# A decoder layer's down projection: results formed in place, twelve slots in reserve, one tile of f split per step, chunks of 10, 12, 12 and 10 row tiles

## The chip, the cores and the metric

The kernel runs on one core of one Trainium2 chip. The metric is the device time of one execution in microseconds; the time before is the median of three runs, 2716.6 us (2716.36 to 2725.06). A difference of about 0.3% is what a measurement of this kernel can tell from none.

## The reference, cut to what matters

One layer of a decoder: a normalised and modulated input, two attention branches with gates, an output projection, then a feed-forward part. The change touches the feed-forward part and a routine which the gates use too. In float32, with 512 tokens, a width of 2048 and an inner width of 5632:

```python
u = h @ w_up                                   # (512, 2048) @ (2048, 11264)
conv = b_conv + sum(w_conv[j] * up[:, j:j + S])  # causal, three taps
gate, val = split(conv)
f = silu(gate) * val                           # (512, 5632)
x = x + gt_f * (f @ w_down)                    # (512, 5632) @ (5632, 2048)
```

The kernel holds everything transposed: rows are channels (128 partitions), columns are the 512 tokens.

## The kernel before, in words

**Numbers as hi and lo.** A float32 matrix is multiplied as three products of rounded halves. `split` (L114, L115) makes them: ACT writes `hi`, a rounded copy, and DVE writes `lo`, the source less `hi`. Each weight tile and each operand tile goes through it. For one pair of K slabs PE then does hi x hi, hi x lo and lo x hi (L1065, L1066, L1067).

**Seven products for eight.** Gates, up projection (except its first group) and down projection run in `seven`, a scheme with seven block products in place of eight. A `Pair` is two output tiles of 128 rows and 512 tokens, computed as a 2 x 2 block of (row tile) x (token half); K is the number of row tiles in each half of the inner dimension. The seven steps have the order p1, p7, p6, p2, p5, p4, p3, and each has an operand set of K blocks of 128 x 256: r11, t3, t2, r21, t1, t4, r22 (`KINDS`). The weights of a pair are four blocks, loaded by SP into five `raw` buffers (in most of the up projection partly into slots), combined by DVE (`comb`, L965) and split into three `whi`/`wlo` buffers. The weights of a step are prepared two steps ahead (`AHEAD`).

**Evictions.** A pair has two PSUM banks of 512 columns, used as three halves X, Y and Z. p1 starts X, p6, p5 and p3 add to X; p7 starts Y, p4 adds to it; p2 uses Z. After each step its half is read: e1, e7, e6 and e3 are copies by ACT (`copy`, L969 with the per-row factor of the down projection, L971 without), e2, e5 and e4 are additions by DVE (`plus`, L975 and L977). Before, e1 and e7 write the two halves of a scratch tile `s` and e6 half of another one, `s6`; e2, e5 and e4 read them and write `u1` and `u2`.

**Slots.** Operands, f, results and scratch live in 81 tiles of 128 x 512, handed out by `get` from the front of a queue and returned by `put` to its end. The order in which they are handed out is fixed when the program is written; an instruction that writes a slot waits for the slot's last readers. A result tile of the down projection is read by an accumulating DMA into `x1_d` (L1526, issued by POOL); in the last chunk it is added to x1 (L1523) and stored.

**f and its chunks.** The up projection yields f, 44 row tiles. For two of them `f_out` computes the sums that the scheme needs and writes them to DRAM (L1373, L1382). The down projection goes over f in four chunks, `DH` = 6, 6, 5, 5 pairs of row tiles, and in each chunk over eight pairs of output tiles, so 56 steps a chunk. A chunk needs seven sets. A set is DH blocks of 128 x 256 in three tiles (with five blocks the third tile is half full), loaded by SP (`load_set`, L1459, one DMA per block) and split into six slots, which stay until the set's last use in the chunk's last pair.

**What sets the order.** After each step `hook` returns the operands that have had their last use and calls `ahead`, which splits and loads sets of the next chunk. `split_set` splits all three tiles of a set. It does so when at least 2 n + 8 slots are free (n is 3; 6 in place of 8 for the first chunk), at every fourth step for the first four sets of a chunk, and at any step in the last eight steps before the chunk is needed. Loads are written while fewer than three sets wait and n + 8 slots are free. The program's text is not the order of the queues: a planner orders each engine's instructions by its own model of time, so an instruction can stand in its queue ahead of ones that are written earlier. Each engine then runs its queue in that order.

## Time and profile before

| | |
|---|---|
| median of three runs | 2716.6 us (2716.36 to 2725.06) |
| profiled execution | 2718.77 us, its span 2716.3 us, mean granted clock 0.99 |
| PE busy | 2620.4 us (96%) |
| DVE busy | 2184.6 us (80%) |
| ACT busy | 1285.3 us (47%) |
| POOL busy | 270.5 us (10%) |
| DMA | 464.33 MB, mean 171 GB/s |

A row of a group of instructions gives line, engine, operation, names of output and inputs, shapes and count, then busy time and the mean duration of one in ns, then the idle time of the engine just before them with what ended it. A row of waits says who waited for what: us in total, times, longest. A row of the timeline gives start and length in us, engine, line, operation, names, and in brackets the idle time before it. A row of a stretch gives for each engine the busy time and the number of instructions in it. `x<-slot` is the accumulating DMA of a result tile, `slot<-f` a load of f.

### The profile page before, as it was taken

What the parts mean: (1) busy time and instruction counts of PE and PEld (TensorE: products, weight loads), DVE (VectorE), ACT (ScalarE), POOL (GpSimd) and SP (SyncE); (2) the same over time, 40 slices, a digit from 0 to 9 for tenths busy, and PEclk for the clock granted to TensorE, in tenths of its full rate; (3) what the DMA queues carried; (4) which work ended last, traced back from release to release, by engine and by line L of the source; (5) the groups of instructions that cost most, each with busy time, mean ns of one, the idle gap of its engine ahead of it and who ended that gap; (6) DMA issues with size and microseconds to landing.
All of it is one profiled execution on the core that took longest, in us unless ns stands there. A gap on an engine that the chain in (4) does not pass through costs nothing. (4 is left out here: it accounts for less than half of the span.)

```text
span 2716.3 us, 45517 instructions
## 1 busy us (share of the span) xinstructions
PE 2620.4 (96%) x17200; PEld 2351.7 (87%) x17200; DVE 2184.6 (80%) x3669; ACT 1285.3 (47%) x2069; POOL 270.5 (10%) x495
## 2 busy tenths in 40 slices
PE   6999999998999999999999999999999989898999
PEld 5777687778997767788789999999999989898989
DVE  7877966688878667983778989989889897777778
ACT  4333434334444455332545555555555464545554
POOL 1001011110032222110100000000000001011110
PEclk8999899999999999999999999999999999999999
DMA  9943136664585578962333333433433466766574
GB/s 343 341 153 98 34 110 213 197 214 156 190 269 164 161 255 288 323 238 93 132 114 124 134 137 113 147 120 114 148 120 128 140 205 154 187 141 173 137 206 125
DMA packets 236241, 464.33 MB, mean 171 GB/s; under 512 B 24331, under 2 KB 85413, under 8 KB 236021
## 3 DMA queue, kind: packets, MB, share of 16 engines
q1 hardware_dynamic: 199348, 368.79, 42.5%
q0 software_dynamic: 36640, 92.63, 11.7%
q8 instruction: 134, 2.20, 0.3%
q14 instruction: 87, 0.70, 0.1%
q10 hardware_dynamic: 32, 0.01, 0.0%
HBM read 397.11 MB, written 64.23 MB: 170 GB/s over the span
## 5 line engine op out<-in xcount | busy, mean ns | idle before, releaser
L1065 PE MATMUL bank<-slot,whi 128*128 128x256 f32 x3920 | 1109.9, 283 | 49.4 <-ACT slot L969 17.0
L1067 PE MATMUL bank<-slot,wlo 128*128 128x256 f32 x3920 | 1101.6, 282 | 8.3 <-DVE wlo L115 8.2
L1066 PE MATMUL bank<-slot,whi 128*128 128x256 f32 x3920 | 1104.4, 282 | 0.4 <-DVE slot L115 0.4
L1065 PEld LDWEIGHTS bank<-slot,whi 128*128 128x128 f32 x3920 | 743.4, 190 | 62.4 <-ACT slot L969 22.2
L1067 PEld LDWEIGHTS bank<-slot,wlo 128*128 128x128 f32 x3920 | 739.9, 189 | 10.8 <-DVE wlo L115 10.3
L1066 PEld LDWEIGHTS bank<-slot,whi 128*128 128x128 f32 x3920 | 741.7, 189 | 0.8 <-DVE slot L115 0.6
L114 ACT ACTIVATE whi<-raw 128x1024 fp32r<-128x1024 f32 (+2 forms) x458 | 424.6, 928 | 500.1 <-PE bank L1066 385.5
L115 DVE TENSOR_TENSOR wlo<-raw,whi 128x1024 fp32r<-128x1024 f32 (+2 forms) x458 | 482.1, 1056 | 61.7 <-ACT whi L114 59.6
L106 ACT ACTIVATE whi<-raw 128x1024 fp32r<-128x1024 f32 (+4 forms) x182 | 187.3, 1032 | 396.0 <-PE bank L120 201.8
L107 DVE TENSOR_TENSOR wlo<-raw,whi 128x1024 fp32r<-128x1024 f32 (+4 forms) x182 | 215.7, 1186 | 146.4 <-ACT whi L106 146.0
L965 DVE TENSOR_TENSOR raw<-raw,raw 128x1024 f32<-128x1024 f32 (+2 forms) x252 | 264.8, 1051 | 61.8 <-DMA raw<-in_w_down 33.3
L119 PE MATMUL bank<-wlo,slot 128*128 128x512 f32 (+2 forms) x768 | 297.4, 388 | 0.9 <-DVE wlo L107 0.9
L118 PE MATMUL bank<-whi,slot 128*128 128x512 f32 (+2 forms) x768 | 290.1, 391 | 4.7 <-ACT slot L385 4.3
L120 PE MATMUL bank<-whi,slot 128*128 128x512 f32 (+2 forms) x768 | 293.3, 385 | 0.0
L118 PE MATMUL bank<-slot,whi 128*128 128x512 f32 (+1 forms) x656 | 261.2, 405 | 3.3 <-ACT slot L1346 2.3
L119 PE MATMUL bank<-slot,whi 128*128 128x512 f32 (+1 forms) x656 | 263.1, 402 | 0.7 <-DVE slot L687 0.7
L120 PE MATMUL bank<-slot,wlo 128*128 128x512 f32 (+1 forms) x656 | 257.5, 401 | 0.0
L118 PEld LDWEIGHTS bank<-whi,slot 128*128 128x128 f32 x768 | 145.9, 190 | 36.1 <-ACT slot L385 4.3
L723 DVE SCALAR_TENSOR_TENSOR slot<-slot,c_act,slot 128x512 f32<-128x512 f32 x203 | 148.9, 745 | 33.9 <-DMA slot<-in_w_ada 32.8
L119 PEld LDWEIGHTS bank<-wlo,slot 128*128 128x128 f32 x768 | 146.2, 190 | 30.0 <-DVE wlo L107 1.4
L120 PEld LDWEIGHTS bank<-whi,slot 128*128 128x128 f32 x768 | 144.6, 188 | 29.0 <-issue 0.5
L114 ACT ACTIVATE whi<-slot 128x512 fp32r<-128x512 f32 x204 | 127.0, 630 | 79.4 <-PE bank L1066 63.8
(292 smaller groups left out, 3004.6 us busy)
## 6 DMA issues: line engine op xcount, KB each, us to landing
slot<-in_w_ada SPq DMA_DIRECT2D x344, 256.0 KB, 5.7
raw<-in_w_ups SPq DMA_DIRECT2D x126, 512.0 KB, 4.4
raw<-in_w_in SPq DMA_DIRECT2D x50, 512.0 KB, 3.6
raw<-in_w_down SPq DMA_DIRECT2D x64, 384.0 KB, 3.1
raw<-in_w_down SPq DMA_DIRECT2D x64, 320.0 KB, 3.4
slot<-f SPq DMA_DIRECT2D x154, 128.0 KB, 3.3
slot<-in_w_ups SPq DMA_DIRECT2D x68, 256.0 KB, 2.6
f<-slot POOLq DMA_DIRECT2D x66, 256.0 KB, 5.2
```

The source lines that it names most:

```text
L106: A.activation(hi, raw[:, :w], AF.Copy)
L107: V.tensor_tensor(lo, raw[:, :w], r32(hi), ALU.subtract)
L114: A.activation(dst_hi, src, AF.Copy)
L115: V.tensor_tensor(dst_lo, src, r32(dst_hi), ALU.subtract)
L118: PE.matmul(o, lh, rh, start=first, stop=False)
L119: PE.matmul(o, lh, rl, start=False, stop=False)
L120: PE.matmul(o, ll, rh, start=False, stop=last)
L723: V.scalar_tensor_tensor(acc, ts[i], c_act[:, k:k + 1], acc, op0=ALU.mult, op1=ALU.add)
L965: V.tensor_tensor(part(o, x, y), part(a, x, y), part(b, x, y), op)
L1065: PE.matmul(o, wh[:, ks], rh, start=first and k == 0, stop=False, skip_group_check=True)
L1066: PE.matmul(o, wh[:, ks], rl, start=False, stop=False, skip_group_check=True)
L1067: PE.matmul(o, wl[:, ks], rh, start=False, stop=last, skip_group_check=True)
```

## The change

Four things change together.

- `seven`: the scratch tiles `s` and `s6` are gone. e1 takes `u1` and copies X into its left half, e7 takes `u2` and copies Y into its right half, e6 copies into the left half of `u2`; e2, e5 and e4 add to these halves in place.
- `split_set` becomes `split_tile`, which splits one tile.
- `ahead` splits a tile at every third step, and at each of the last eight steps before the chunk and the first steps of it, when 14 slots are free (8 for the first chunk). It splits a second tile in a step when otherwise some set would come too late. Loads need n + 12 free slots. The window opens 54 steps before the chunk instead of 50.
- The chunks are 5, 6, 6 and 5 pairs of row tiles; the host packs w_down accordingly.

```diff
-    DH=(6, 6, 5, 5),
+    DH=(5, 6, 6, 5),
...
-            def plus(o, b, g, x):
+            def plus(o, b, g):
                 if g is not None:
-                    V.scalar_tensor_tensor(o, b, g, x, op0=ALU.mult, op1=ALU.add)
+                    V.scalar_tensor_tensor(o, b, g, o, op0=ALU.mult, op1=ALU.add)
                 else:
-                    V.tensor_tensor(o, b, x, ALU.add)
+                    V.tensor_tensor(o, b, o, ALU.add)
...
             def e1():
-                E["s"] = get()
-                copy(E["s"][:, :HT], X, g1)
+                E["u1"] = get()
+                copy(E["u1"][:, :HT], X, g1)

             def e7():
-                copy(E["s"][:, HT:], Y, g2)
+                E["u2"] = get()
+                copy(E["u2"][:, HT:], Y, g2)

             def e6():
-                E["s6"] = get()
-                copy(E["s6"][:, :HT], X, g2)
+                copy(E["u2"][:, :HT], X, g2)

             def e2():
-                E["u1"] = get()
-                plus(E["u1"][:, :HT], Z, g1, E["s"][:, :HT])
+                plus(E["u1"][:, :HT], Z, g1)

             def e5():
-                E["u2"] = get()
-                plus(E["u2"][:, HT:], X, g2, E["s"][:, HT:])
-                put(E["s"])
+                plus(E["u2"][:, HT:], X, g2)

             def e4():
-                plus(E["u2"][:, :HT], Y, g2, E["s6"][:, :HT])
-                put(E["s6"])
+                plus(E["u2"][:, :HT], Y, g2)
...
-    def split_set():
-        c, n, ts = coming.popleft()
-        for i, t in enumerate(ts):
-            hi, lo = getr(), getr()
-            w = min(T, (DH[c] - 2 * i) * HT)
-            split(hi[:, :w], lo[:, :w], t[:, :w])
-            put(t)
-            held_by[c][n] += [hi, lo]
-            ops[c][n] += [(hi[:, o:o + HT], lo[:, o:o + HT]) for o in range(0, w, HT)]
+    def split_tile():
+
+        c, n, ts = coming[0]
+        t = ts.pop(0)
+        if not ts:
+            coming.popleft()
+        w = T if ts or DH[c] % 2 == 0 else HT
+        hi, lo = getr(), getr()
+        split(hi[:, :w], lo[:, :w], t[:, :w])
+        put(t)
+        held_by[c][n] += [hi, lo]
+        ops[c][n] += [(hi[:, o:o + HT], lo[:, o:o + HT]) for o in range(0, w, HT)]
...
-        if c > last or left > 50:
+        if c > last or left > 54:
             return
-        n, spare = need(c), 8 if c else 6
-        if coming and coming[0][0] <= c and len(free) >= 2 * n + spare and (left <= 8 or left % 4 == 0 and made[0] < 4):
-            made[0] = (made[0] + 1) % 7
-            split_set()
-        while todo and todo[0][0] <= c and len(coming) < (3 if c or len(free) > 15 else 1) and len(free) >= n + spare:
+        spare = 12 if c else 6
+        near = left <= 8
+        if coming and len(free) >= 2 + spare and (near or left % 3 == 0):
+            split_tile()
+
+            n = (DH[c] + 1) // 2
+            at = KINDS.index(coming[0][1]) if coming else 7
+            if any(len(coming[0][2]) + n * (i - at) > left + i - 2 for i in range(at, 7)):
+                split_tile()
+        while todo and todo[0][0] <= c and len(coming) < (3 if c or len(free) > 15 else 1) \
+                and len(free) >= (DH[c] + 1) // 2 + spare:
             load_set()
...
-        ahead(0 if (coming or todo or [(0,)])[0][0] == c else 56 - r, c + 1)
+        ahead(-r if (coming or todo or [(0,)])[0][0] == c else 56 - r, c + 1)
```

More of the change, by code (lines that the diff above doesn't have):

```diff
@@ L1460, in load_set @@
         coming.append((c, n, ts))
-    def split_set():
-        c, n, ts = coming.popleft()
-        for i, t in enumerate(ts):
-            hi, lo = getr(), getr()
-            w = min(T, (DH[c] - 2 * i) * HT)
-            split(hi[:, :w], lo[:, :w], t[:, :w])
-            put(t)
-            held_by[c][n] += [hi, lo]
-            ops[c][n] += [(hi[:, o:o + HT], lo[:, o:o + HT]) for o in range(0, w, HT)]
-    def need(c):
-        return (DH[c] + 1) // 2
-    made = [0]
+    def split_tile():
[9 more added lines that the diff above has]
+        ops[c][n] += [(hi[:, o:o + HT], lo[:, o:o + HT]) for o in range(0, w, HT)]
     def ahead(left, last):
         c = (coming or todo or [(9,)])[0][0]
-        if c > last or left > 50:
+        if c > last or left > 54:
             return
-        n, spare = need(c), 8 if c else 6
-        if coming and coming[0][0] <= c and len(free) >= 2 * n + spare and (left <= 8 or left % 4 == 0 and made[0] < 4):
-            made[0] = (made[0] + 1) % 7
-            split_set()
-        while todo and todo[0][0] <= c and len(coming) < (3 if c or len(free) > 15 else 1) and len(free) >= n + spare:
+        spare = 12 if c else 6
[8 more added lines that the diff above has]
+                and len(free) >= (DH[c] + 1) // 2 + spare:
             load_set()
@@ L1583 @@
             dn, k0, ds = a.reshape(DFF // (2 * P), 2, P, D), 0, []
-            for n in (6, 6, 5, 5):
+            for n in (5, 6, 6, 5):
                 b = dn[k0:k0 + n].transpose(1, 0, 2, 3).reshape(2 * n * P, D)
```

## The prediction

> **What bounds the kernel now.** I read the page's slices first, then the busy times by stretch, then the waits, then single queues.

> ```profile
> span 2716.3 us, 45517 instructions
> PE   6999999998999999999999999999999989898999
> ```

> PE is at 90% or more in nearly every slice; the visible dents of the second half stand in the last fifth, the down projection. The stretches below are cut at first matmuls, found by counting (a pair of output tiles is 7 products of 3 x 6 matmuls with twelve row tiles, 3 x 5 with ten). Columns: stretch, length, busy time and instructions of PE, PEld, DVE, ACT, POOL, granted clock, DMA share, GB/s.

> ```profile
> 2176.30:2196.20 19.90, 19.90 (x171) 19.90 (x170) 18.28 (x24) 11.85 (x17) 1.62 (x3) 1.00 0.51 159
> 2196.20:2222.40 26.20, 21.94 (x171) 21.53 (x170) 24.30 (x35) 17.13 (x28) 0.54 (x1) 0.93 0.81 249
> 2222.40:2244.40 22.00, 17.76 (x128) 16.79 (x127) 20.60 (x31) 14.16 (x23) 2.51 (x4) 0.92 0.75 241
> 2244.40:2261.80 17.40, 15.65 (x129) 15.17 (x128) 12.03 (x16) 8.01 (x12) 0.87 (x1) 1.00 0.61 170
> 2277.20:2307.00 29.80, 29.80 (x254) 29.80 (x253) 22.94 (x29) 15.38 (x23) 3.50 (x5) 1.00 0.59 142
> 2307.00:2341.70 34.70, 30.92 (x255) 30.10 (x254) 24.51 (x33) 16.31 (x25) 3.30 (x5) 1.00 0.59 145
> 2341.70:2358.60 16.90, 15.15 (x129) 14.95 (x128) 15.09 (x22) 14.01 (x25) 0.93 (x2) 1.00 0.87 232
> 2358.60:2395.90 37.30, 31.51 (x255) 30.20 (x254) 27.87 (x39) 16.32 (x25) 4.30 (x5) 1.00 0.64 170
> 2395.90:2440.60 44.70, 44.70 (x380) 44.70 (x379) 33.98 (x43) 22.75 (x34) 5.07 (x6) 1.00 0.61 142
> 2440.60:2474.30 33.70, 30.84 (x254) 30.03 (x253) 24.17 (x33) 16.19 (x25) 3.24 (x5) 1.00 0.60 145
> 2474.30:2491.80 17.50, 15.20 (x128) 14.99 (x127) 16.42 (x26) 13.38 (x25) 1.00 (x2) 1.00 0.83 219
> 2491.80:2524.10 32.30, 26.45 (x213) 25.32 (x212) 21.59 (x34) 14.48 (x25) 3.43 (x4) 1.00 0.66 172
> 2524.10:2563.60 39.50, 38.03 (x317) 37.45 (x316) 30.11 (x45) 20.26 (x34) 5.15 (x7) 1.00 0.61 140
> 2563.60:2592.40 28.80, 26.23 (x213) 25.21 (x212) 20.70 (x32) 14.55 (x26) 3.88 (x5) 1.00 0.63 147
> 2592.40:2607.80 15.40, 13.47 (x107) 12.63 (x106) 12.96 (x22) 9.92 (x19) 6.59 (x11) 1.00 0.93 261
> 2607.80:2624.10 16.30, 14.18 (x108) 13.75 (x107) 11.46 (x18) 6.52 (x11) 3.99 (x6) 0.93 0.74 214
> 2624.10:2712.00 87.90, 87.90 (x736) 87.67 (x735) 74.08 (x109) 44.91 (x75) 1.07 (x2) 0.99 0.45 138
> ```

> Where no f is split, PE never stops: three pairs with K=6 take 44.7 (14.9 each), the last seven with K=5 87.9 (12.56 each), the up pair at 2176 19.9. Against these floors the rest loses: **start** (last up pair, first two down pairs) 26.2-19.9 + 22.0-14.9 + 17.4-14.9 = 15.9; **three handovers** (last pair of a chunk, first two of the next; of the third handover one pair only, its second runs at the floor) 16.9+37.3-44.7 = 9.5, 17.5+32.3-40.0 = 9.8, 15.4+16.3-25.1 = 6.6; **inside the chunks** 34.7-29.8 = 4.9, 33.7-29.8 = 3.9, and 39.5-37.7 + 28.8-25.1 = 5.5, with 0.5 in the third pair: 14.8. In all 56.6 us, the most that this change can take away.

> ```profile
> PE bank L1065 <- ACT slot L969: 17.0, 18, 2.3
> DVE slot L115 <- DMA x<-slot: 16.7, 8, 3.0
> ACT slot L114 <- DMA x<-slot: 11.2, 7, 2.8
> PE bank L1065 <- DVE slot L975: 10.9, 13, 1.8
> PE bank L1065 <- ACT whi L114: 8.1, 5, 4.2
> PE bank L1067 <- DVE wlo L115: 4.8, 5, 1.8
> ```

> The waits from 2209 on name the mechanism. PE waits 27.9 us for an eviction (L969, L975) and 12.9 for split weights: the products share bank half X, so p6 cannot add to X until ACT has copied it, one product later. ACT and DVE are what is late, and they are late because f splits (`slot`, L114 and L115) stand before evictions: some wait for the accumulating DMA that still reads their slot, some come in a burst. One of each, on ACT:

> ```profile
> 2342.90 1.14 ACT L114 ACTIVATE slot<-slot 128x512 fp32r<-128x512 f32 x2
> ...
> 2344.68 0.62 ACT L114 ACTIVATE slot<-slot 128x512 fp32r<-128x512 f32 x1
> ...
> 2345.55 1.67 ACT L114 ACTIVATE slot<-slot 128x512 fp32r<-128x512 f32 x3
> 2347.68 0.63 ACT L114 ACTIVATE slot<-slot 128x512 fp32r<-128x512 f32 x1 [0.46 <-DMA x<-slot]
> 2348.22 0.83 ACT L114 ACTIVATE whi<-raw 128x768 fp32r<-128x768 f32 x1
> ```

> Seven tiles in 5.4 us, with weights and evictions between and behind them.

> **The change, part by part.** *Work.* Matmuls, weights, evictions, accumulating DMAs and f bytes stay: 22 slabs of two row tiles before and after, and with ten row tiles as with twelve three tiles per set, so 84 splits.

> *Results in place.* Two slots per pair instead of four, held 6 and 5 steps instead of 12 slot-steps in four tiles. The add reads the tile that it writes. Price by two rows of equal shape:

> ```profile
> L115 DVE TENSOR_TENSOR slot<-slot,slot 128x512 fp32r<-128x512 f32 x49 | 32.9, 685 | 9.9 <-DMA x<-slot 5.7 <-ACT slot L114 4.0
> L1523 DVE TENSOR_TENSOR slot<-slot,slot 128x512 f32<-128x512 f32 x16 | 10.9, 684 | 1.1 <-ACT slot L969 1.1
> L115 DVE TENSOR_TENSOR slot<-slot,slot 128x256 fp32r<-128x256 f32 x14 | 5.7, 421 | 15.4 <-DMA x<-slot 11.0 <-ACT slot L114 4.4
> ```

> 684 ns in place (L1523) against 685: nothing. No wait is added, since ACT's copy into that half comes a product or more before DVE's add. What changes is the rotation: the two scratch slots per pair that came free at once are gone, and a pair returns only the two slots that its accumulating DMAs still read.

> *The reserve.* A set of three tiles needed 2x3+8 = 14 free slots, one tile needs 2+12 = 14. Inside a chunk the end state is the same: 81 - 42 (operands) - 18 (three sets split) - 9 (three loaded) = 12, less a result tile. Loads want 15 free instead of 11, so they are written later. Followed step by step, a chunk has the next one's splits or loads directed to slots last read by an accumulating DMA at five moments before (of the previous chunk's last pair, then of pairs 1, 5, 6, 7) and five after (last, 1, 4, 5, 7) for splits; for loads at two before, three after (pairs 2, 6, 7). The queue order is not the program's: a split that is written in the last pair (from 2341.7) stands in ACT's queue two pairs early, at the very landing that it needs:

> ```profile
> 2310.39 0.63 ACT L114 ACTIVATE slot<-slot 128x512 fp32r<-128x512 f32 x1 [2.05 <-DMA x<-slot]
> ```

> So distance in the program doesn't buy quiet, and I count 0 for the 14.8 inside the chunks (bounds: 0 if each wait stays, -14.8 if all go). One more load wait per chunk costs SP:

> ```profile
> SPq L1459 <- DMA x<-slot: 21.0, 5, 5.9
> ```

> 4.2 us each, and SP's weight loads stand behind it. The stretches from 2307, 2440 and 2563, in which some of these stand, lose 4.9, 3.9 and 3.7 in two pairs, mostly to splits; I give a load's wait 1 us of that: 3 x 1 = +3 (bounds 0 and 3 x 4.2 = 12.6).

> *One tile per step.* Before, four sets (12 tiles) are written in four consecutive steps of the last pair; after, 7 in the last pair and 5 in the first five steps of the next, each behind its step's eviction. A K=6 pair keeps DVE busy 33.98/3 = 11.3 of 14.9, a K=5 pair 74.08/7 - 2 x 0.684 = 9.2 of 12.56. Seven tiles at 0.685 make 16.1 and 14.0: over by about 1.2; five in the next pair make 14.7 and at most 12.6: they fit. Floor per handover 1.2; the second pair's stop (a landing, as above; 2.5 by the 17.40 row) stays in the first two. Of the rest of 9.5, 9.8, 6.6, that is 5.8, 6.1 and 5.4, which a burst with DMA at 0.83 to 0.93 causes together, I take three quarters off: 4.4+4.6+4.0 = -13.0 (bounds 0, if the order stays a burst, and -17.3).

> *Chunks of 10, 12, 12, 10.* The first chunk needs 35 loads instead of 42 and its third tiles are half wide, 7 x (0.685-0.421) = 1.8 of DVE; its last two sets move behind the last up pair. DVE over the start was busy 24.3+20.6+12.0 = 56.9 against PE's 49.7, so 7.2 of the 15.9 is too much work for DVE. After: 56.9 - 1.8 - 2 x (11.3-9.2) = 50.9, against 19.9+25.1 = 45.0, over by 5.9, less what the next chunk's nine hoisted tiles (9 x 0.685, loaded while the first chunk starts) no longer press in. I take the start at 10, DVE's excess and half of the 15.9-7.2 that was not DVE's work: -5.9 (bounds -2, DVE's 1.8 alone, and -12, if only those 4 are left).

> ```profile
> slot<-f SPq DMA_DIRECT2D x61, 128.0 KB, 3.3
> raw<-in_w_down SPq DMA_DIRECT2D x8, 384.0 KB, 5.2
> ```

> These issues, from 2196 to 2244, say why it isn't more: 61 f loads keep the DMA engines at 0.75 to 0.81, and a weight tile lands after 5.2 us.

> The clock lost 7% of 26.2, 8% of 22.0 and 7% of 16.3, 4.7 us, in the three stretches with the long stops (0.93, 0.92, 0.93); it is part of the 56.6. [...]

> **Sum.** -13.0 - 5.9 + 3 = -15.9 against this execution's 2718.8 (span 2716.3 and 2.5 around it), which stands 2.2 above the median of 2716.6. On the median: 2716.6 - 15.9 = **2700.7**, taken as 2700.

> **Rivals.** *A, the landings go too.* If single tiles find their slots long landed, the 14.8 goes with no load wait added: -13.0 - 5.9 - 14.8, and 3 more at the start, half-way to its bound, = -36.7, **2680**. For it: 15 split waits of 27.9 us, the largest group. Against: the split that stood two pairs early, at 2310.

> *B, the burst stays.* The queues' order follows free slots, not the text, and the slots of a handover come free at the same products as before. Then only the start gains, between its -2 and -5.9, about -4: **2713**. For it: the same split. Against: the burst at 2342.9 stands where it is written.

> *C, slower: SP held at landings.* In-place results leave only slots that end in an accumulating DMA, and three load moments per chunk meet one, of pairs 2, 6 and 7. SP then stands at 4.2 us, weight loads behind it, DVE's comb waits, PE too. If four such waits more reach PE whole (16.8) and DVE, full at 16.1 of 14.9, returns nothing at the handovers, with the start's -5.9: +10.9, **2727**. It decides from the point where the added waits cost PE more than the gains, 5.9 with the handovers returning nothing, 18.9 with them. For it: PE has no reserve for late weights at a handover (5.2 us landing). Against: buffers allow weights to be loaded ahead.

> **How the numbers follow.** Forecast 0.46 (its own range 2690 to 2707), A 0.20, B 0.14, C 0.20. What can be told from no change is 0.3%, 8.1 us: below 2708.5 faster, 0.46+0.20 = 0.66; B same, 0.14; C slower, 0.20. The range goes from a little below A to C: 2675 to 2727.

> **What would show it.** Right: between the last and second pair of chunks the stops of 2 to 5 us shrink to about 1, ACT shows one f split between evictions; the first chunk starts at about 2216; DMA waits of splits stay near 28 us; pairs inside chunks still lose 4 to 5 us per chunk. Wrong: those pairs run at 14.9 (A), several f splits in a row in ACT's queue at the handovers (B), SP's waits for `x<-slot` well above 21 us with DVE waiting for `raw` above its

> ```profile
> DVE raw L965 <- DMA raw<-in_w_down: 33.3, 34, 3.0
> ```

> (C). The gates, which use the same code, must stay at their length; a shift there would be an effect that I have not counted.

## The result and the profile after

The changed kernel takes 2751.0 us (median of 4 runs, 2745.16 to 2755.26) beside 2719.15 us of the kernel before on the same chip: a ratio of 1.0116, 95% interval 1.0096 to 1.0137. It is slower by 1.2%, where 2700 us had been forecast, and it lies outside the range of 2675 to 2727. Its profiled execution has a span of 2753.5 us against 2716.3.

The page of the changed kernel, its busy slices (tenths) of PE:

```profile
span 2753.5 us, 45502 instructions
PE   6999999999999999999999999999999989888999
```

The dents are still in the last fifth. The stretches of the changed kernel, cut as those of before at first matmuls (stretch, length, busy time and instructions of PE, PEld, DVE, ACT, POOL, granted clock, DMA share, GB/s):

```profile
2182.80:2205.60 22.80, 20.45 (x171) 20.04 (x170) 19.63 (x26) 11.21 (x15) 1.62 (x3) 1.00 0.41 135
2205.60:2227.90 22.30, 20.41 (x170) 20.01 (x169) 20.96 (x32) 16.02 (x29) 0.54 (x1) 1.00 0.79 243
2227.90:2247.70 19.80, 14.79 (x107) 14.12 (x107) 17.44 (x30) 11.91 (x22) 2.20 (x4) 0.91 0.87 262
2247.70:2269.00 21.30, 16.06 (x108) 15.39 (x107) 13.62 (x21) 9.01 (x16) 1.16 (x2) 0.84 0.42 94
2269.00:2340.60 71.60, 65.21 (x527) 63.97 (x526) 49.84 (x72) 33.51 (x57) 8.54 (x10) 0.98 0.60 147
2340.60:2359.20 18.60, 14.55 (x107) 13.35 (x106) 15.64 (x25) 12.74 (x23) 1.71 (x2) 0.97 0.72 195
2359.20:2398.40 39.20, 33.45 (x254) 32.66 (x254) 30.00 (x40) 18.38 (x29) 4.20 (x5) 0.93 0.63 178
2398.40:2484.20 85.80, 78.68 (x632) 77.86 (x632) 58.37 (x73) 37.80 (x57) 8.61 (x11) 0.96 0.57 139
2484.20:2504.70 20.50, 16.92 (x128) 16.51 (x127) 17.25 (x26) 13.91 (x26) 0.86 (x1) 0.92 0.81 225
2504.70:2544.80 40.10, 34.84 (x255) 33.94 (x254) 27.45 (x37) 17.75 (x29) 4.31 (x5) 0.87 0.50 129
2544.80:2627.80 83.00, 77.41 (x633) 76.39 (x632) 57.39 (x73) 37.06 (x56) 8.44 (x10) 0.98 0.57 140
2627.80:2646.20 18.40, 15.43 (x128) 15.02 (x127) 14.87 (x23) 10.68 (x19) 8.06 (x16) 1.00 0.88 254
2646.20:2660.20 14.00, 12.71 (x108) 12.51 (x107) 10.02 (x16) 6.74 (x11) 3.29 (x5) 1.00 0.85 240
2660.20:2749.30 89.10, 87.87 (x737) 87.25 (x735) 74.19 (x110) 44.82 (x75) 0.00 (x0) 1.00 0.41 131
```

Against the floors of the prediction (19.9 for a pair of the up projection, 14.9 with K=6, 12.56 with K=5) the excess is:

| place | before | after | from the rows of after |
|---|---|---|---|
| start | 15.9 | 21.3 | 22.8 + 22.3 - 39.8, then 19.8 + 21.3 - 25.1 |
| three handovers | 25.9 | 36.2 | 18.6 + 39.2 - 42.4 = 15.4; 20.5 + 40.1 - 44.7 = 15.9; 18.4 + 14.0 - 27.5 = 4.9 |
| inside the chunks | 14.8 | 28.6 | 71.6 - 62.8 = 8.8; 85.8 - 74.5 = 11.3; 83.0 - 74.5 = 8.5 |
| last seven pairs | 0 | 1.2 | 89.1 - 87.9 |
| sum | 56.6 | 87.3 | |

Of the 37.2 us that the span grew, 30.7 stand here, in all three places. The up projection without its last two pairs takes 816.5 - 45.1 = 771.4 us against 813.8 - 46.1 = 767.7. From the first matmul of the gates' pairs to that of the up projection it is 795.7 against 792.9; in the other kernels this lies between 789.3 and 797.0 whatever their edit, so 2.8 us there can't be told from none. PE is busy for 2636.5 us instead of 2620.4, with 17200 matmuls in both: 16.1 of the 37.2 us are the same matmuls taking longer, which fits the lower granted clock (0.84 to 0.98 in nine of the fourteen stretches above; last section), the rest is time in which PE stands.

The waits of the changed kernel from 2222 us to the end (who waits for what: us in total, times, longest), then the waits of SP's queue from 2195 us:

```profile
DVE raw L965 <- DMA raw<-in_w_down: 38.9, 34, 3.4
PE bank L1061 <- ACT slot L969: 27.5, 15, 4.1
ACT slot L114 <- DMA slot<-f: 25.1, 13, 3.8
ACT slot L114 <- DMA x<-slot: 14.8, 6, 4.1
PE bank L1061 <- DVE slot L975: 13.5, 12, 2.4
DVE slot L115 <- DMA x<-slot: 12.2, 5, 4.6
PE bank L1061 <- ACT whi L114: 8.4, 8, 2.7
PE bank L1063 <- DVE wlo L115: 4.8, 3, 3.1
```

```profile
SPq L1455 <- DMA x<-slot: 39.2, 15, 6.1
```

Three things moved. SP waits 39.2 us for landings of the accumulating DMAs, 15 times, instead of 21.0 and 5. ACT waits 25.1 us for f itself (`slot<-f`); before, the row was 7.6 in 4 waits (below). The splits' own waits for landings are the same in sum, 14.8 + 12.2 = 27.0 against 27.9, but in 11 waits instead of 15, up to 4.6 us instead of 3.0: what a wait of 4 us does to PE, the timeline below shows. The waits of before that the prediction did not show, from 2209 us:

```profile
ACT slot L114 <- DMA slot<-f: 7.6, 4, 4.7
```

How one landing becomes a stop of PE, in the timeline of the changed kernel at the second handover (start, length, engine, line, operation, in brackets the idle time before it and what ended it), first ACT and DVE, then PE:

```profile
2514.47 0.63 ACT L114 ACTIVATE slot<-slot 128x512 fp32r<-128x512 f32 x1 [4.14 <-DMA x<-slot]
...
2513.41 0.69 DVE L115 TENSOR_TENSOR slot<-slot,slot 128x512 fp32r<-128x512 f32 x1 [4.64 <-DMA x<-slot]
2514.02 0.95 DVE L965 TENSOR_TENSOR raw<-raw,raw 128x768 f32<-128x768 f32 x1
2514.89 1.82 DVE L115 TENSOR_TENSOR wlo<-raw,whi 128x768 fp32r<-128x768 f32 x2
...
2515.90 0.58 PE L1063 MATMUL bank<-slot,wlo 128*128 128x256 f32 x1 [3.10 <-DVE wlo L115]
2516.28 0.42 PE L1061 MATMUL bank<-slot,whi 128*128 128x256 f32 x1
2516.49 0.42 PE L1062 MATMUL bank<-slot,whi 128*128 128x256 f32 x1
```

DVE and ACT both stand at the head of their queues with a split whose slot an accumulating DMA still reads. The weight split (L115 at 2514.89) stands behind it on DVE, its data long there (ACT wrote the two `whi` that go with it at 2508.04 and 2509.12), and PE waits 3.10 us for that.

### The profile page after: what moved, and what is told of

Its sections match the earlier page's. It is cut to its first block, busy times and chain, and to the rows that moved or that the text cites. A ratio compares the mean times of both kernels' runs of the same rounds, so it can differ in the third digit from the quotient of the medians.

```text
span 2753.5 us, 45502 instructions
## 1 busy us (share of the span) xinstructions
PE 2636.5 (96%) x17200; PEld 2366.9 (86%) x17200; DVE 2188.4 (79%) x3669; ACT 1284.4 (47%) x2069; POOL 270.7 (10%) x495
## 5 line engine op out<-in xcount | busy, mean ns | idle before, releaser
L1061 PE MATMUL bank<-slot,whi 128*128 128x256 f32 x3920 | 1117.3, 285 | 70.1 <-ACT slot L969 27.5
L114 ACT ACTIVATE whi<-raw 128x1024 fp32r<-128x1024 f32 (+2 forms) x458 | 424.5, 928 | 475.8 <-PE bank L1062 373.1
L115 DVE TENSOR_TENSOR wlo<-raw,whi 128x1024 fp32r<-128x1024 f32 (+2 forms) x458 | 483.7, 1058 | 72.0 <-ACT whi L114 69.8
L965 DVE TENSOR_TENSOR raw<-raw,raw 128x1024 f32<-128x1024 f32 (+2 forms) x252 | 265.0, 1052 | 67.0 <-DMA raw<-in_w_down 38.9
L723 DVE SCALAR_TENSOR_TENSOR slot<-slot,c_act,slot 128x512 f32<-128x512 f32 x203 | 149.2, 747 | 27.1 <-DMA slot<-in_w_ada 26.1
L120 PEld LDWEIGHTS bank<-whi,slot 128*128 128x128 f32 x768 | 145.3, 189 | 28.8 <-issue 0.4
L114 ACT ACTIVATE whi<-slot 128x512 fp32r<-128x512 f32 x204 | 128.3, 629 | 80.7 <-PE bank L1062 68.4
## 6 DMA issues: line engine op xcount, KB each, us to landing
raw<-in_w_down SPq DMA_DIRECT2D x64, 384.0 KB, 4.0
slot<-f SPq DMA_DIRECT2D x154, 128.0 KB, 3.5
```

Source lines behind the costliest of these rows:

```text
L114: A.activation(dst_hi, src, AF.Copy)
L115: V.tensor_tensor(dst_lo, src, r32(dst_hi), ALU.subtract)
L120: PE.matmul(o, ll, rh, start=False, stop=last)
L723: V.scalar_tensor_tensor(acc, ts[i], c_act[:, k:k + 1], acc, op0=ALU.mult, op1=ALU.add)
L965: V.tensor_tensor(part(o, x, y), part(a, x, y), part(b, x, y), op)
L1061: PE.matmul(o, wh[:, ks], rh, start=first and k == 0, stop=False, skip_group_check=True)
```

## The experiments

The theory after the result (R in the expectations): reusing a result's slot while its accumulating DMA still reads it costs the time; forming results in place took away the two scratch slots per pair that came free without a landing. The rivals: f lands late for its splits, because loads wait for 15 free slots (L); the order of the chunks; the single tiles (T), with which the order of the queues changes. Every kernel computes the whole result. All ratios are to the kernel before on the same chip, with 95% intervals.

### One part alone, on the kernel before

In place only (`plus` and e1 to e4 as in the diff of the change, nothing else):

```diff
-                copy(E["s"][:, :HT], X, g1)
+                copy(E["u1"][:, :HT], X, g1)
...
-                plus(E["u1"][:, :HT], Z, g1, E["s"][:, :HT])
+                plus(E["u1"][:, :HT], Z, g1)
```

> The kernel before with the results formed in place, nothing else changed. Undoing this part in the changed kernel was worth 0.6%. Theory R (in-place results leave only slots that an accumulating DMA still reads): alone it costs too, about 8 us at chunk ends and 3 us in the up projection, 2733 us against 2722; SP's waits for x<-slot rise above 30 us. Theory I (the parts hurt only together, through the order of the queues): within 5 us of before.

Measured: 1.0069 [1.0044, 1.0094]. SP's waits in this kernel:

```profile
SPq L1455 <- DMA x<-slot: 38.3, 15, 4.7
```

That is as many as in the changed kernel, with the old loads, sets and chunks. The pairs inside the chunks lose 29.3 us, as much as in the changed kernel (28.6), and the handovers 23.6, no more than before.

Chunks of 10, 12, 12, 10 only:

```diff
-    DH=(6, 6, 5, 5),
+    DH=(5, 6, 6, 5),
```

> The kernel before with chunks of 10, 12, 12, 10 row tiles, nothing else changed. The prediction's step for it was -5.9 us at the start. If that holds alone: about 2716 us against 2722, the start's excess of 15.9 us near 10. If two chunks of twelve in the middle cost (undoing it in the changed kernel was worth 0.4%): about 2732 us, with the loss at the second and third handover.

Measured: 1.0020 [1.0007, 1.0033]. The start doesn't get shorter: last up pair 8.1 above its floor, first two down pairs 7.2 and 3.0, together 18.3 against 15.9. The larger loss in this kernel's profile is at the handovers, 32.4 us instead of 25.9, most of it at the first, where the first pairs with K=6 follow the last with K=5 (15.4 instead of 9.5).

Later loads only (15 free slots instead of 11 for all chunks but the first):

```diff
-        ... and len(free) >= n + spare:
+        ... and len(free) >= n + (12 if c else 6):
```

> The kernel before with loads that need 15 free slots instead of 11, nothing else changed. Undoing this in the changed kernel moved little (0.2%). Theory L, as far as it is left: 2 to 5 us slower, about 2726 us, with ACT's waits for f above 7.8 us. Otherwise within 3 us of before.

Measured: 1.0057 [1.0036, 1.0078]. The waits of this kernel from 2195 us, SP's and ACT's:

```profile
SPq L1459 <- DMA x<-slot: 41.0, 11, 7.6
```

```profile
ACT slot L114 <- DMA slot<-f: 28.6, 18, 5.5
```

Loads that are written later stand longer for landings, and f then comes late: 28.6 us of waits on ACT instead of 7.8 over the same stretch of before. The loss stands at the handovers, 37.8 us instead of 25.9, and at the start, 22.2 instead of 15.9.

Single tiles, with their window and the rule for late ones, loads as before:

```diff
-            split_set()
+        if coming and len(free) >= 2 + spare and (near or left % 3 == 0):
+            split_tile()
...
-        while ... and len(free) >= n + spare:
+        while ...
+                and len(free) >= (DH[c] + 1) // 2 + (8 if c else 6):
```

> The kernel before with f split one tile per step, and the new window and lateness rule, nothing else changed: four-slot results, chunks of 12, 12, 10, 10, loads at 11 free slots. The prediction's step for it was -13.0 us at the handovers. If that holds alone: about 2709 us against 2722. Theory T (single tiles come late, splits stand in ACT's queue for a load): about 2735 us, ACT's waits for f above 20 us and the handovers above 12 us each instead of 9.5.

Measured: 0.9984 [0.9968, 1.0001]. The handovers come down from 25.9 to 21.1 us, and the pairs inside the chunks go up from 14.8 to 20.6. SP's waits for landings rise here too, at no loss of time:

```profile
SPq L1459 <- DMA x<-slot: 32.8, 13, 5.1
```

The four parts add to +0.69 + 0.57 + 0.20 - 0.16 = +1.30%, near the +1.16% of the whole.

### One part taken back, on the changed kernel

Scratch tiles back:

> The changed kernel with one part undone: the two scratch tiles s and s6 are back, results are no longer formed in place. Theory R: the scratch slots, free at once, come between the accumulated ones again; SP's waits for x<-slot fall from 39.2 to about 21 us and the time to about 2730 us. Theory L and theory T: little changes, 2745 to 2755 us, or a little worse, because scratch takes slots from the loads.

Measured: 1.0059 [1.0038, 1.0081]. Chunks back:

> The changed kernel with one part undone: chunks of 12, 12, 10, 10 row tiles again. If the new order of chunks helps the start as the prediction had it, this is some 6 us slower than the changed kernel, about 2757 us. If the order costs, because two chunks of twelve now stand in the middle, it is faster, about 2740 us. Theories L, R and T have no part in it: within 8 us of 2751.

Measured: 1.0072 [1.0045, 1.0099]. Loads at 11 free slots again (`+ (8 if c else 6)` in place of `+ spare`):

> The changed kernel with one part undone: loads of f need n + 8 = 11 free slots again instead of n + 12 = 15; single tiles, in-place results and the new chunks stay. Theory L (the larger reserve holds back the loads; f comes late, splits stand in ACT's queue for it, 25.1 us against 7.6 before, and SP stands at landings, 39.2 us against 21.0): most of the loss goes, about 2728 us, ACT's waits for f back under 12 us. Theory R (in-place results leave only slots whose last reader is an accumulating DMA): little changes, 2745 to 2755 us. Theory T (single tiles come late by their own order): little changes, 2745 to 2755 us.

Measured: 1.0095 [1.0060, 1.0130]. Whole sets split by the old rule:

> The changed kernel with one part undone: f is split a whole set of three tiles at a time, with the rule of before (every fourth step, at most four sets early), loads still need 15 free slots. Theory T: back to about 2725 us, the last and first pairs of chunks lose 10 us a handover again instead of 15. Theory L: the late loads stay, 2745 to 2760 us. Theory R: 2745 to 2755 us.

Measured: 1.0055 [1.0037, 1.0074]. Each takes back 0.57, 0.44, 0.21 and 0.61% of the 1.16 (1.83 together), the 0.21 within what the intervals leave open. The parts are not independent: single tiles, which alone cost nothing, are worth 0.6% to undo in the changed kernel. Taking back the loads alone left SP at 37.7 us in 14 waits for landings, so with results in place the loads' rule is not what makes SP stand. But neither is in place alone: with the scratch tiles back SP stands longer than in the changed kernel, where theory R expected some 21 us:

```profile
SPq L1459 <- DMA x<-slot: 52.7, 14, 5.8
```

The pairs inside the chunks still lose 26.1 us then (in a profiled run of 2746.05 us; the median is 2739.17). With whole sets back they lose 18.0, with the loads or the chunks back 28.9 and 29.7. So single tiles bring on the loss inside the chunks as well as results in place do, and the sum of SP's waits does not follow the time: 32.8 us at 0.9984, 38.3 at 1.0069, 52.7 at 1.0059.

### The landings taken away

Results of the down projection get four slots of their own, used in turn; they never return to the common slots. A slot's next result comes two pairs later, some 25 to 30 us, long after a landing (4.8 us by the median of `x<-slot` in the issues of before). The edit, on each base (`u2` like `u1`; on the kernel before the lines stand in e2 and e5):

```diff
+    ring = deque()
+    def result(p):
+        if p.scale is None:
+            return get()
+        if not ring:
+            ring.extend(get() for _ in range(4))
+        ring.rotate(-1)
+        return ring[-1]
...
-                E["u1"] = get()
+                E["u1"] = result(p)
...
-            put(*us, *x1)
+            put(*x1)
```

On the kernel with results in place only:

> The kernel before with results formed in place, and the down projection's result tiles taken from four slots of their own in turn, so that no slot that an accumulating DMA reads is handed to a load or a split; the common stock has 77 slots. Theory R (the loss of 0.69% of in-place results is the landings of accumulating DMAs at which splits and loads stand): the waits of splits and of SP for x<-slot go to about zero and the loss with them, 2705 to 2722 us. Rival S (the loss comes from the order of the queues or from fewer slots): it stays near 2738 us or grows, since four slots fewer are free.

Measured: 0.9976 [0.9962, 0.9989], 0.93% below the same kernel without own slots. On the changed kernel:

> The changed kernel with the four slots of their own for result tiles. Theory R: the in-place part of the loss goes, 2751 to about 2735 us or below; what the later loads and the chunks cost stays, so ACT's waits for f stay above 20 us. Rival S: 2750 us or more.

Measured: 1.0000 [0.9988, 1.0011], 1.16% below the changed kernel. ACT's waits for f fall too, below the 20 us that were expected (numbers below). On the kernel with results in place and single tiles:

> The parts that did no harm put together: single tiles, loads at 11 free slots, chunks of 12, 12, 10, 10, results in place with the four slots of their own. If theory R holds and the parts add up: the 0.16% of the single tiles and the landings together, about 2700 us, faster than both kernels. Otherwise not below 2715 us.

Measured: 0.9984 [0.9969, 0.9999], 2716.6 us. The 2700 that adding the parts would give did not come. On the kernel before:

> The kernel before, scratch tiles kept, with the four slots of their own for result tiles and nothing else. Theory R: the 27.9 us of splits' waits and SP's 21.0 us go, the pairs inside chunks (14.8 us of excess) run nearly free: about 2708 us against 2721. Rival S: four slots fewer make it slower, 2725 to 2735 us.

Measured: **0.9919 [0.9897, 0.9941]**, a median of 2700.3 us. This is the fastest of all, faster than both kernels of this case. Two of its stretches (columns as above), the second to seventh pair of the first and of the second chunk:

```profile
2250.00:2339.20 89.20, 89.20 (x756) 89.20 (x755) 70.46 (x89) 47.00 (x70) 10.42 (x13) 1.00 0.62 147
2374.40:2463.80 89.40, 89.40 (x758) 89.40 (x757) 70.34 (x90) 46.72 (x70) 10.17 (x12) 1.00 0.62 146
```

Six pairs at 14.9 without a gap on PE, and in no kernel with own slots does SP, ACT or DVE wait for a landing. The changed kernel with own slots has the same inside its second chunk, and not at the handover (third to seventh pair, then the last one, 7.3 us above its floor):

```profile
2388.10:2462.70 74.60, 74.60 (x633) 74.60 (x631) 57.25 (x71) 36.95 (x55) 8.57 (x11) 1.00 0.60 142
2462.70:2484.90 22.20, 16.77 (x128) 16.36 (x127) 17.48 (x27) 14.07 (x26) 0.85 (x1) 0.92 0.84 229
```

So the loss inside the chunks is the landings', shown by taking them away on four bases: 2.0 us are left there with in place only (29.3 without own slots), 3.6 in the changed kernel (28.6), 3.6 with in place and single tiles, 1.9 on the kernel before (14.8).

It is not the price of the change, though, since the kernel before has these landings too and gains 0.81% itself. With own slots in place costs 0.9976 - 0.9919 = 0.57% (+-0.26), beside 0.69% without, and the whole change still +0.8% (+-0.25): most of the difference of the two kernels goes another way. Of the 20.5 us between the profiled spans of the changed kernel and the kernel before, each with own slots, 14.7 stand at the handovers (34.7 and 20.0). With in place only against the kernel before, each with own slots, inside and handovers are the same; the start takes 21.3 instead of 15.8, and the up projection without its last two pairs 772.4 instead of 767.2. The timeline of the changed kernel with own slots in its pair at 2462.70, ACT and PE, shows what stands there now:

```profile
2471.24 0.63 ACT L114 ACTIVATE slot<-slot 128x512 fp32r<-128x512 f32 x1 [3.51 <-DMA slot<-f]
...
2473.03 0.46 ACT L979 ACTIVATE slot<-bank,mod 128x256 f32<-128x256 f32 x1
...
2473.54 0.58 PE L1071 MATMUL bank<-slot,whi 128*128 128x256 f32 x1 [4.30 <-ACT slot L979]
```

The same stop, with another DMA at its head: the split waits for f to land, the eviction (L979) stands behind the split, and PE behind that. ACT's waits for f from 2222 us are 17.6 us in 12 here, and 5.6 in 4 in the kernel before with own slots.

### The parts again, without the landings

Each on the kernel before with own slots (0.9919). In place in gates and up only, then in down only (`inplace = p.scale is None`, and `is not None`):

> The kernel before with four slots of their own for the down projection's results; results are formed in place in the gates and the up projection alone, the down projection keeps its scratch tiles. Without any in-place part this was 0.9919 of before, with all of it 0.9976. Theory U (in place costs in the up projection, where the scratch tiles were the only slots not read by a DMA that writes f, and weights and f are loaded into what comes next): near 0.997, up projection 3 us longer, the start of the down projection some 6 us. Rival V (the cost is in the down projection): near 0.992.

> The same with results in place in the down projection alone, scratch tiles in the gates and the up projection. Theory U: near 0.992. Rival V: near 0.997, with the loss at the handovers.

Measured: 0.9954 [0.9937, 0.9971] and 0.9943 [0.9925, 0.9961]: +0.35 and +0.24% (each +-0.28). The first is a loss; the second can't be told from none. In the up projection, which has no accumulating DMA, the waits show another cost. SP's waits from 1408 to 2222 us in the kernel before with own slots and, after it, with up in place; then DVE's and PE's in the same two:

```profile
SPq L962 <- DVE slot L1367: 297.4, 46, 12.3
...
SPq L962 <- DVE slot L987: 5.0, 2, 2.7
...
DVE slot L975 <- DMA raw<-in_w_ups: 33.5, 24, 4.2
PE bank L1075 <- DVE slot L987: 2.1, 6, 0.5
```

```profile
SPq L962 <- DVE slot L975: 214.8, 31, 8.6
SPq L962 <- DVE slot L989: 116.2, 20, 7.9
...
DVE slot L975 <- DMA raw<-in_w_ups: 58.1, 31, 4.4
PE bank L1086 <- DVE slot L989: 9.1, 18, 1.7
```

Part of the up weights is loaded into slots, so those loads wait for whatever held the slot before. With scratch tiles SP's largest wait for a slot ends with DVE's convolution (L1367); in place, with the combining of weights (L975) and with a pair's eviction by DVE (L989). DVE then waits 25 us longer for weights that are loaded into slots, and PE 7 us longer for DVE's evictions. The up projection takes 821.3 us in this kernel and 813.8 without; over all profiles it takes 816.0 to 821.3 us with results in place there, but for one at 813.1, and 807.8 to 814.6 with scratch tiles. The one at 813.1 is the kernel with results in place and nothing else, where the same wait of DVE grows too (49.6 us, 36.1 in the kernel before, which takes 813.8). That these waits make the up projection longer is argued, not tried.

Nor is the 0.35% the up projection's alone. In the same two profiles the down projection takes 477.4 us against 470.5, and the gates' eight pairs, first matmul to last, 169.9 against 178.6. In all ten profiles with results in place there the gates' pairs take 169.9 to 174.6 us, in the ten with scratch tiles 175.4 to 180.9; what follows them up to the up projection takes most of the gain back, for a reason that no run shows.

Own slots on the changed kernel with loads at 11 free slots, and single tiles with own slots:

> The changed kernel with the four slots of their own and with loads at 11 free slots instead of 15. With the slots alone it was 1.0000 of before, its loss at the handovers (the last pairs of chunks lose 6.3, 7.3 and 4.9 us), where splits wait 20.7 us for f. Theory L: the loads of the fourth to last sets come earlier, these waits fall below 12 us, the time to 0.996. If the loads' moment does not matter any more: 0.999 to 1.001.

> The kernel before with the four slots of their own and with single tiles (scratch, loads at 11, chunks of 12, 12, 10, 10). The slots alone: 0.9919. If single tiles help the handovers as the prediction had it (-13 us), 0.987; if they do nothing, 0.991 to 0.993; if splits come late by them, 0.995 or more with the last pairs of chunks longer than 2.5 to 4 us above their floor.

Measured: 0.9987 [0.9973, 1.0001], nothing that can be told from 1.0000 without the edit, and 0.9936 [0.9920, 0.9952], nothing that can be told from 0.9919. In the first ACT's waits for f stay at 20.9 us, where theory L had them below 12. Single tiles gain nothing at the handovers with the landings gone either: 27.3 us against 20.0 in the two profiles. Last, chunks of 10, 12, 12, 10 and later loads, each alone with own slots:

> Before with four result slots of its own for the down projection (0.9919) and chunks of 10, 12, 12 and 10 row tiles, nothing else changed. Theory (the landings of accumulating DMAs are what the order of chunks pays for): without them the order costs nothing, 0.992 +- 0.002. Rival (the first chunk has one set fewer to hide behind and the start is no shorter, whatever the slots do): the +0.20% that the order alone measured stays, 0.994 or above.

> Before with four result slots of its own (0.9919) and loads only where 15 slots are free instead of 11. Theory (a late load costs because it is directed to a slot whose accumulating DMA has not landed, and SP stands): with own slots there is no such wait, SP shows no wait for x<-slot, and the +0.57% of later loads alone shrinks to at most 0.1%: 0.992 to 0.993. Rival (a late load costs because f then lands late for its split): f waits on ACT above 20 us and 0.996 to 0.998.

Measured: 0.9951 [0.9937, 0.9964] and 0.9950 [0.9937, 0.9962], +0.32 and +0.31% (+-0.25). For the chunks the rival holds: their cost does not go through the landings. For the loads the theory is half right: there is no wait for a landing on SP any more, and of 0.57% about half is left, with f late on ACT:

```profile
ACT slot L114 <- DMA slot<-f: 19.5, 17, 3.9
```

Against 9.8 us in 9 waits in the kernel before with own slots, over the same stretch. With and without landings the cost of later loads is 0.31 and 0.57; the intervals overlap, so the share is an estimate.

## Why the prediction was wrong

The steps added to -15.9 us; the same places measured +30.7.

**Handovers, -13.0.** The largest miss. Measured 36.2 - 25.9 = +10.3. Single tiles alone bring 4.8 us there and give back 5.8 inside the chunks, so rival B's point (free slots set the order, not the text) fits the tiles. What turned the gain into a loss are two parts that the step did not charge there: later loads alone cost 37.8 - 25.9 = 11.9 us at the handovers, with f late on ACT, and the new chunks alone 32.4 - 25.9 = 6.5. Own slots take little of it away (34.7 are left in the changed kernel), so most of this loss is not the landings'. Why the order of chunks costs there is open.

**Inside the chunks, 0.** The step counted five moments with landings for splits before and after, gave bounds of 0 and -14.8, and so allowed no loss. Measured 28.6 - 14.8 = +13.8. The sum of the splits' waits was right (27.0 against 27.9); the longest grew from 3.0 to 4.6 us, with the evictions and weight splits of the queue behind it. The prediction had said that "the two scratch slots per pair that came free at once are gone", and priced it at nothing. In place alone takes this loss to 29.3 us, single tiles alone to 20.6, and own slots take it to 1.9 to 3.6.

**In-place price, nothing.** Right for the instruction (the 96 additions of L975 have a median of 477 ns before and of 479 in place), wrong for the edit, 18.8 us at 0.69%. In the profile of in place alone nearly all of it is inside the chunks, at the landings. With own slots 0.57% is left all the same, in the profiles at the start and in the up projection. In place in the gates and the up projection alone costs 0.35% with own slots, a part that the prediction didn't price. The gates, which it said must stay at their length, got shorter by 2.1 us (174.6 and 176.7).

**Load waits, +3, bound 12.6.** Mis-sized, and the bound too low. Later loads alone cost 0.57%, 15.5 us. The step priced SP's stand at a landing and forgot what is late next: f, with ACT's queue behind it.

**Start, -5.9.** Measured +5.4, and the first chunk starts at 2227.9 us, not at about 2216. The step shortened DVE's work and left out that a chunk with K=5 also gives less time to hide it in; the chunks alone show 18.3 us at the start instead of 15.9, the later loads alone 22.2. That the shorter pairs are the reason for the first is argued, not tried.

**The clock.** The prediction put the 4.7 us of missing clock down to three stretches with long stops. Two of the three have no stop over 1.95 us; the third has one of 4.24. In the changed kernel PE stops for over 1.5 us 14 times from 2196 us on, instead of 8 times, 13 stretches of 3.41 us have a granted clock of 0.50 (2235.15 to 2593.55 us) instead of 3 (from 2218.88, 2225.71 and 2621.66 us), and PE is busy 16.1 us longer with the same matmuls, a term that the sum did not have.

**Rival C** named a right place (results in place leave only slots that end in a landing, SP stands) and both of its marks came: SP's row at 39.2 against 21.0, DVE's wait for `raw` at 38.9 against 33.3. But the first mark does not tell the kernels apart, as the runs above show. Its price, 2727, was too small: it kept the start's -5.9 and let the handovers stay as they were. It is also not the whole: of 1.16% some 0.8 stay with own slots. What stays is in place in the gates and the up projection, the chunks and late f, each measured at about 0.3%; they do not add exactly, and which of them meets which at a handover is open. So is whether in place in the down projection costs anything without landings (0.24 +- 0.28).

## What to carry to other kernels

A buffer that is freed by a slow reader (here an accumulating DMA, 4.8 us from issue to landing by the median) isn't free: when an edit saves buffers, look at what the remaining ones end in, not at how many there are. Where evictions and splits stand in one engine's queue, a late DMA at its head can stop what is behind it: here a split's wait of 4.64 us on DVE became a stop of 3.10 us on PE. So read the longest wait beside the sum: the sum of the splits' waits stayed (27.9 and 27.0 us) and the longest grew (3.0 and 4.6). Four slots set aside for the results of an accumulating DMA were worth 0.8% here, more than any change to the order of the work.

## What the runs showed of the hardware

```profile
2224.74 0.39 PE L1065 MATMUL bank<-slot,whi 128*128 128x256 f32 x1 [1.95 <-ACT whi L114]
...
2222.30:2225.71 3.41, 1.46 (x12) 1.26 (x12) 2.00 (x3) 2.66 (x5) 0.00 (x0) 1.00 0.83 250
2225.71:2229.12 3.41, 3.41 (x19) 3.41 (x18) 3.41 (x6) 3.41 (x7) 0.00 (x0) 0.50 0.86 254
```

```profile
2387.26 0.38 PE L1065 MATMUL bank<-slot,whi 128*128 128x256 f32 x1 [2.29 <-ACT slot L969]
...
2382.72:2386.13 3.41, 2.26 (x20) 2.05 (x18) 2.01 (x3) 0.85 (x1) 0.00 (x0) 1.00 0.90 248
2386.13:2389.54 3.41, 2.28 (x19) 2.28 (x20) 1.99 (x3) 1.87 (x4) 0.00 (x0) 1.00 0.13 51
```

The shorter stop lies within one stretch, of which PE works 1.46 of 3.41 us, and the next stretch has half the clock (0.50). The longer one lies across an edge, PE works two thirds of either stretch (2.26 and 2.28 of 3.41), and the clock stays at 1.00. A stop of 1.80 us that ends at 2621.36 lies within one stretch again (1.61 of 3.41 us worked), and half the clock follows. Cut on that grid from 2196 us on, the traces of the kernel before and of the changed one have 12 stretches at full clock in which PE stood for more than 0.55 of the time, and each was followed by half clock; none in which it stood for 0.52 or less was. In between both occur: the stretch from 2502.19 us in the kernel before (1.60 of 3.41 us worked) was followed by full clock, the one with 1.61 above by half. So in these two traces where a stop fell on the grid counted beside its length.

At half clock the matmuls follow each other at 0.21 us (2516.28 to 2516.49 above; the clock granted from 2516.00 to 2521.00 is 0.50) instead of 0.12 (756 in 89.20 us). Lengths times the clock that was missing, over the stretches of the first section, make about 22 us, against 5.6 in the rows of before; these are upper bounds, since they include time in which PE stood anyway. PE's busy time, 16.1 us longer, fits the difference.
